# A one-core hybrid layer on Trainium2: buffers and priorities around the gates, the recurrence's decays and the first attention loads

## The chip, the cores and the metric

The kernel runs on one NeuronCore of one Trainium2 chip. The metric is the device time of one execution in microseconds (us). The engines that matter are the matrix engine TensorE (PE, with its weight loads shown apart as PEld), VectorE (DVE), ScalarE (ACT), GpSimd (POOL), and the queues that issue transfers: SyncE's (SP) and POOL's. Operands lie in the on-chip memory (SBUF), matmul results in PSUM, whose eight banks are shared out among pools of buffers.

## The reference

One layer of a streaming encoder over 512 tokens of width 1024, all in float32:

```python
h = rms_norm(x, norm_mix)
u_pool, u_lru, q, k, v, g_logits = split(h @ w_in)       # 1024 x 8192
gates = sigmoid(g_logits + b_gate)                        # three branches
y_pool = pool_mixer(u_pool)        # causal means over 2, 4, 8, 16 tokens, then a linear map
y_lru  = rglru_mixer(u_lru)        # width-4 conv, gates r and i, h = a*h + sqrt(1-a^2)*i*x
y_sb   = stick_breaking_attention(rms_norm(q), rms_norm(k), v)   # 8 heads of 128
merged = sum(gates[b] * (y_b @ w_branch[b]) for b in 3)
x = x + merged @ w_out
h2 = rms_norm(x, norm_ffn)
x = x + (silu(h2 @ w_ffn_gate) * (h2 @ w_ffn_up)) @ w_ffn_down   # width 2816
```

## The kernel before

Every float32 product is made of three matmuls in a rounded format: each operand is split into a high part (ACT copies it with rounding) and a low part (DVE subtracts the high part), and high*high, high*low and low*high are added up in PSUM. So each set of weights costs one transfer, one copy on ACT (`whi`, L141) and one subtraction on DVE (`wlo`, L142) before PE can use it; the weight pool `wp` has three buffers each for the raw weights, the high and the low parts. Some large products (q, k, v, the gates of branch 2, the projection of branch 2, most of the feed-forward) use a scheme of seven block products in place of eight, called "seven" in the code, with sums of blocks of weights and of inputs made on DVE or by adding transfers.

The program is written in order, stage by stage, and a scheduler puts it in order on each engine: it takes ready instructions by priority, which is the place in the program, and `tc.high_priority(n)` counts an instruction as n places earlier. A tile of a pool with a tag takes one of that tag's buffers, and its first writer waits until the buffer's last tile is done with. Small side tasks are put in two lists, `bg` and `abg`; `tick()`, called after every 12 or so matmuls of the main products, takes the next of each. The stages are:

1. Input scaling; gates of branch 0 (`gate_store`, L601); the scaled input `HH`, `HL`; block differences T1 to T4 (`prepare_t`, L568; `diff_h`, `split_t`).
2. The recurrent branch, four chunks of channels c: the projection (`lru_chunk`, L636), the convolution into `xc` (L642 to L651), its split (`xch`, `xcl`, L656, L657), the gate matmuls `lg` with tanh on ACT (L667 to L672), a tanh into `lt` (L679), the exponentials `lru_exp` (L697) and the root of the same tanh (L700, which needs another function table on ACT), the decay `lru_decay` (L705 and its complement, L707 on DVE for c < 2 and L709 on ACT for c of 2 and 3), the input (L713, L714), the scan (L720) and the store of its two halves (`lru_store`). Between the chunks the gates of branch 1 are made (`gate1`). The decay overwrites the tanh `t`, which the root has read before.
3. v, k and q as token-major products, in that order (`tok_product`, L827), with squares for the norms of k and q (`post`, L793); then the gates of branch 2 (`tx`, `ty`, L895).
4. The pool branch's projection in the group order 1, 0, 3, 2 (`pool_chunk`), whose results ACT copies out of PSUM (`evac_u`, L981) into slots, with the eight heads of attention as tasks in `abg` (`head_tasks`: the loads `at`, the transposes `pq`, the scores `z`, the transposes `pw`, the output `py`), followed by the projections of branches 1 and 0 (`branch`, L312 to L314 as `ps_br`), for which the recurrent branch's result is loaded into the space of HH and HL (L1196).
5. The projection of branch 2, the output projection, the feed-forward part.

In stages 1 to 3 the pool `ap0` holds tiles of 4 KB with the tags b (13 buffers), w (8) and t (8). The ring `m` of the pool `mp` has four such buffers and lives throughout; T1 to T4 use it first, later the merged branches. The space of `ap0` is taken by the slots and loads of stage 4 (`slot`, `slot_ld`) once the stages before are done.

High and low weights lie in buffers of 1152 elements, 128 more than they need; `OFF` and `STEPS` shift the start of the weights of certain products by 0, 4, 8, 12 and then 16 elements. An unused tile `pad` of 41 elements shifts all that lies behind it.

Of the kernel before, what the change touches and what calls it, by code (L numbers as in the profile page):

```python
# [16 lines left out]
P = 128  # L17
# [16 lines left out]
AHEAD = 200  # L34
PAD = 41


OFF = 16
STEPS = (0, 4, 8, 12)
NAW, NAT, NAB = 8, 8, 13  # L40
# [27 lines left out]
def layer_kernel(ctx: ExitStack, tc: tile.TileContext, x, xt, vecs, w_in, w_qkv7, w_gate7, w_pool, w_rg, w_ig,  # L68
# [6 lines left out]
    mp = ctx.enter_context(tc.tile_pool(name="mp", bufs=4))  # L75
    wp = ctx.enter_context(tc.tile_pool(name="wp", bufs=3))
    late = ctx.enter_context(ExitStack())
    hstack = ctx.enter_context(ExitStack())
# [50 lines left out]

    def weight_tiles(nh, nl, o=0):  # L130
        return [wp.tile([P, 1024 + 128], F32R, tag=tag, name=n)[:, o:o + 1024]
                for tag, n in (("whi", nh), ("wlo", nl))]

    def split_w(raw, shape, n, o=0):
        hi, lo = weight_tiles("whi" + n, "wlo" + n, o)
        if len(shape) == 3:
            hi, lo = (t.rearrange("p (a b) -> p a b", a=shape[1]) for t in (hi, lo))
        else:
            hi, lo = (t.rearrange("p (a b c) -> p a b c", a=shape[1], b=shape[2]) for t in (hi, lo))
        with tc.high_priority(60):  # L140
            act(hi, raw, AF.Copy)  # L141
            dve.tensor_tensor(lo, raw, hi.bitcast(F32), ALU.subtract)  # L142
        return hi, lo
# [58 lines left out]
    def add_seven(un, nm, i):  # L202
        u, pieces, shape = UNITS[un]
        last = i == pieces - 1

        def make(n):
            if nm == "S4":
                r = qraw[u, "12", i]
                dve.tensor_tensor(r, r, qraw[u, "S2", i], ALU.add)
            src = qraw[u, {"S1": "21", "S3": "11", "S4": "12"}.get(nm, nm), i]  # L210
            o = 0
            if u >= 3:
                o = goffs.pop(0) if goffs else OFF
            parts = split_w(src, [P] + list(shape), n, o)
# [12 lines left out]
            return parts  # L227
        specs.append((("seven", u, nm, i), make))

    goffs = list(STEPS)  # L230

# [28 lines left out]
    BNEXT = {"11": ("21", BY), "S1": ("11", BX), "S2": ("12", BX)}  # L260
    boffs = list(STEPS)

# [3 lines left out]
    def add_branch7(u, nm):  # L266
        def make(n):
# [3 lines left out]
            else:  # L271
                t = (BY if nm in ("11", "S3") else BX)[u]
            parts = split_w(t, [P, 2, 4, P], n, boffs.pop(0) if boffs else OFF)
            if nm in BNEXT:
# [19 lines left out]
    def emit_next():  # L294
        i = state["i"]
        if i >= len(specs):
            return
        state["i"] = i + 1
        key, make = specs[i]
        with tc.high_priority(AHEAD if i > 6 else 0):  # L300
            ready[key] = make(str(i))
# [30 lines left out]

    cst.tile([P, PAD], F32, tag="pad", name="pad")
    warm = cst.tile([P, S], BF16, tag="warm", name="warm")
    dve.memset(warm, 1.0)
# [108 lines left out]
    with ExitStack() as first:  # L444
# [12 lines left out]
        for i in range(WARM):  # L457
            nc.tensor.matmul(wps[:, 0, :], warm[:, 0:P], warm, start=True, stop=True)

# [141 lines left out]
        def gate_store(br, c, pss, scaled):  # L601
            gt = b4([2, S], f"gt{br}{c}")
            for j in range(2):
# [88 lines left out]
        def lru_exp(cs):  # L692
            for c in cs:
                for j in range(2):
                    r = lru[c]["r"][:, j, :]
                    ct = 2 * c + j
                    act(r, r, AF.Exp, scale=cneg[:, ct:ct + 1], bias=cneg[:, ct:ct + 1])  # L697
            for c in cs:
                lru[c]["s"] = b4([2, S], f"ls{c}")
                act(lru[c]["s"], lru[c]["t"], AF.Sqrt, scale=0.25)  # L700


        def lru_decay(c):
            e, t = lru[c]["r"], lru[c]["t"]
            dve.scalar_tensor_tensor(t, e, 1.0, t, ALU.add, ALU.mult)  # L705
            if c < 2:
                dve.tensor_scalar(t, t, -1.0, 1.0, ALU.mult, ALU.add)  # L707
            else:
                act(t, t, AF.Identity, scale=-1.0, bias=1.0)  # L709

# [5 lines left out]
        def lru_scan(c):  # L716
            t, s_ = lru[c]["t"], lru[c]["s"]
            h = lru[c]["i"]
# [34 lines left out]
        gate_store(0, 3, pss[3], False)  # L753
        tick(len(bg))

        def gate1(c):
# [22 lines left out]
        gate1(2)  # L779
        for f, c in ((lru_decay, 2), (lru_decay, 3), (lru_input, 2)):  # L780
            step(of(f, c))
        bg.extend(prepare_t())
        gate1(3)
# [9 lines left out]
        def post(t, i, j, r):  # L793
            if t < 2:
                sq = b4([2, 512], f"sq{t}{i}{j}")
                if t == 0:
# [97 lines left out]
        for cc in range(2):  # L894
            tx, ty = b4([2, S], f"gx{cc}"), b4([2, S], f"gy{cc}")  # L895
            if cc:
# [48 lines left out]
    with ExitStack() as mix:  # L945
# [34 lines left out]

        def evac_u(ps, name):  # L981
            u = slot(name)
            act(two(u), in_order(ps), AF.Copy)  # L983
            return u
# [35 lines left out]
        def pool_chunk(g):  # L1020
            pss = chan_chunk(("pool", g), hn, 1)
            us = [evac_u(pss[j], f"up{g}{j}") for j in range(2)]
            for j in range(2):
# [20 lines left out]
        def head_tasks(h):  # L1044
# [4 lines left out]
            def load():  # L1049
                for t in range(3):  # L1050
                    r = slot_ld(f"at{h}{t}", (NS, HD))
                    nc.sync.dma_start(r, qd[t, g][:, hd].rearrange("(b p) c -> p b c", p=P))
                    st["raw", t] = r
# [119 lines left out]
        def queue_attention():  # L1173
# [8 lines left out]
            for p in range(max(todo) + 1):  # L1182
                abg.append(lambda fs=todo.get(p, ()): [f() for f in fs])

        load_pool_weights(0)
        queue_attention()
        for g in POOL:
# [110 lines left out]
    with ExitStack() as ffn:  # L1298
# [114 lines left out]
        made = [0, NDIRECT]  # L1413
        offs = []

# [13 lines left out]
        def make_a(upto):  # L1429
            while made[0] < min(upto, len(steps)):  # L1430
                c, nm = steps[made[0]]
                made[0] += 1
                if (c, nm) == (NDIRECT, "11"):
                    offs.extend(STEPS)
                while made[1] < min(c + 2, DOWN):
# [5 lines left out]
        def split_a(src, n):  # L1441
            o = offs.pop(0) if offs else OFF
            h, l = (t.rearrange("p (w k c) -> p w k c", w=2, k=4)
                    for t in weight_tiles("wh" + n, "wl" + n, o))
            act(h, src, AF.Copy)  # L1445
# [133 lines left out]
        def make_d(upto):  # L1579
            while dmade[0] < min(upto, len(dsets)):  # L1580
                nm, n = dsets[dmade[0]]
                dmade[0] += 1
                if dmade[0] == 1:
                    offs.extend(STEPS)
                dfetch(dmade[0])
# [156 lines left out]
```

## Time and profile before

| | us |
|---|---|
| median of 3 runs | 871.64 |
| lowest, highest | 871.51, 872.29 |
| profiled execution, its time | 872.32 |
| profiled execution, its span in the trace | 870.5 |

The granted TensorE clock was full throughout. In the lines of the profile an engine's instruction is named by its line in the code (L142), its operation and its tiles, written as result<-operands; "[1.4 <-ACT up L983]" says that the engine had been idle for 1.4 us and what ended this. PEq, SPq and so on are the engines' queues. Times of PE's matmuls overlap, since they are pipelined: the distance from start to start is their pace.

### The profile page before, as it was taken

The numbers are of one execution on the slowest core, as the hardware profiler recorded it, in microseconds if no ns is written. First come the engines' busy times: TensorE is split into PE (matmuls) and PEld (weight loads), VectorE is DVE, ScalarE is ACT, GpSimd is POOL, SyncE is SP. The second block draws the span as 40 slices with busy tenths as digits, with TensorE's granted clock in tenths as the row PEclk, the third lists the DMA queues.
The fourth block names the chain that finished last, engine by engine and source line by source line (L and its number), as shares of the span: only waits on it lengthen the run. The fifth ranks groups of instructions, "written<-read, shape, count | busy, mean of one in ns | idle before, by whom it ended". The sixth has DMA issues, their size and how long they took to land.

```text
span 870.5 us, 14271 instructions
## 1 busy us (share of the span) xinstructions
PE 860.6 (99%) x5563; PEld 790.0 (91%) x5563; DVE 741.1 (85%) x961; ACT 523.1 (60%) x727; POOL 91.2 (10%) x130
## 2 busy tenths in 40 slices
PE   9999999999999999999999999999999999999998
PEld 7888878888899888889889998889999999999998
DVE  7899897998796599977988786699998888899974
ACT  7554989557966565565665545464555555755642
POOL 1110002232433101000001100000000000121200
PEclk9999999999999999999999999999999999999999
DMA  9586356798582886644636955345543433797913
GB/s 339 165 287 203 98 167 187 212 324 253 178 275 73 241 243 203 221 122 151 214 103 167 199 172 169 98 139 151 156 111 97 116 104 119 228 240 194 196 42 121
DMA packets 116643, 154.08 MB, mean 177 GB/s; under 512 B 8160, under 2 KB 90080, under 8 KB 116576
## 3 DMA queue, kind: packets, MB, share of 16 engines
q1 hardware_dynamic: 103904, 107.30, 38.4%
q0 software_dynamic: 12528, 45.62, 22.0%
q8 instruction: 43, 0.70, 0.3%
q10 hardware_dynamic: 144, 0.26, 0.1%
q14 instruction: 24, 0.20, 0.1%
HBM read 132.71 MB, written 18.87 MB: 174 GB/s over the span
## 4 chain that ended last, share of the span: by engine, by line
PE 84%; DVE 7%; ACT 5%; DMA 2%; issue 1%; SPq 0%; ACTq 0%; DVEq 0%
PE ps_y L321 11%; PE ps_x L321 8%; PE ps_q L837 7%; PE ps_dy L1661 6%; PE ps_dx L1661 5%; PE ps_br L312 3%; PE ps_br L313 3%; PE ps_br L314 3%; PE ps_bY L1280 2%; PE ps_gate L740 2%; PE ps_gy L321 2%; DVE wlo L142 2%; PE ps_bX L1280 2%; PE ps_gx L321 2%; PE ps_lru L312 1%; PE ps_out L312 1%
## 5 line engine op out<-in xcount | busy, mean ns | idle before, releaser
L141 ACT ACTIVATE whi<-raw 128x1024 fp32r<-128x1024 f32 x69 | 72.9, 1056 | 78.3 <-PE ps_out L313 16.1
L142 DVE TENSOR_TENSOR wlo<-raw,whi 128x1024 fp32r<-128x1024 f32 x69 | 84.3, 1221 | 24.8 <-ACT whi L141 24.3
L142 DVE TENSOR_TENSOR wlo<-qw,whi 128x1024 fp32r<-128x1024 f32 x48 | 58.4, 1220 | 16.5 <-ACT whi L141 16.3
L141 ACT ACTIVATE whi<-qw 128x1024 fp32r<-128x1024 f32 x48 | 50.6, 1054 | 28.8 <-PE ps_q L837 14.8
L1445 ACT ACTIVATE wh_S<-w_S 128x1024 fp32r<-128x1024 f32 x36 | 38.2, 1062 | 30.2 <-PE ps_y L321 18.3
L1565 POOL DMA_DIRECT2D dw<-in_w_down_dram x20 | 17.0, 864 | 306.1 <-DMA dw<-in_w_down_dram 263.8
L1446 DVE TENSOR_TENSOR wl_S<-w_S,wh_S 128x1024 fp32r<-128x1024 f32 x36 | 43.9, 1221 | 3.2 <-ACT wh_S L1445 3.2
L1445 ACT ACTIVATE wh<-w 128x1024 fp32r<-128x1024 f32 x27 | 28.6, 1060 | 29.3 <-PE ps_x L321 9.1
L1446 DVE TENSOR_TENSOR wl<-w,wh 128x1024 fp32r<-128x1024 f32 x27 | 33.0, 1221 | 8.2 <-ACT wh L1445 8.2
L1445 ACT ACTIVATE whdS<-dw 128x1024 fp32r<-128x1024 f32 x20 | 21.2, 1061 | 20.3 <-PE ps_dy L1661 11.2
L1096 DVE TENSOR_TENSOR_SCAN E<-K,ahead 128x512 f32<-128x512 f32 (+3 forms) x32 | 25.4, 814 | 3.9 <-ACT K L1092 3.9
L1446 DVE TENSOR_TENSOR wldS<-dw,whdS 128x1024 fp32r<-128x1024 f32 x20 | 24.2, 1222 | 4.9 <-ACT whdS L1445 4.9
L312 PE MATMUL ps_br<-yHH,whi 128*128 128x512 f32 x64 | 24.6, 385 | 1.4 <-ACT up L983 1.4
L312 PE MATMUL ps_lru<-HH,whi 128*128 128x512 f32 x64 | 24.6, 384 | 0.0
L312 PE MATMUL ps_br<-yph,whi 128*128 128x512 f32 x64 | 24.5, 383 | 0.0
L312 PE MATMUL ps_pool<-HH,whi 128*128 128x512 f32 x64 | 24.5, 383 | 0.0
L312 PE MATMUL ps_gate<-HH,whi 128*128 128x512 f32 x64 | 24.4, 381 | 0.0
L313 PE MATMUL ps_lru<-HL,whi 128*128 128x512 f32 x64 | 24.3, 379 | 0.0
L314 PE MATMUL ps_lru<-HH,wlo 128*128 128x512 f32 x64 | 24.3, 379 | 0.0
L313 PE MATMUL ps_gate<-HL,whi 128*128 128x512 f32 x64 | 24.3, 379 | 0.0
L314 PE MATMUL ps_gate<-HH,wlo 128*128 128x512 f32 x64 | 24.3, 379 | 0.0
L313 PE MATMUL ps_pool<-HL,whi 128*128 128x512 f32 x64 | 24.3, 379 | 0.0
(740 smaller groups left out, 3444.5 us busy)
## 6 DMA issues: line engine op xcount, KB each, us to landing
raw<-in_w_in_dram SPq DMA_DIRECT2D x31, 512.0 KB, 5.3
qw<-in_w_qkv_dram SPq DMA_DIRECT2D x24, 512.0 KB, 6.8
dw<-in_w_down_dram POOLq DMA_DIRECT2D x20, 512.0 KB, 9.2
w<-in_w_ffn_gate_dram SPq DMA_DIRECT2D x36, 256.0 KB, 3.7
w<-in_w_ffn_up_dram SPq DMA_DIRECT2D x36, 256.0 KB, 4.2
raw<-in_w_branch_dram SPq DMA_DIRECT2D x16, 512.0 KB, 3.9
qw<-in_w_qkv_dram POOLq DMA_DIRECT2D x12, 512.0 KB, 8.1
qd<-r POOLq DMA_DIRECT2D x12, 512.0 KB, 6.7
```

The lines of the kernel that those rows point to most:

```text
L141: act(hi, raw, AF.Copy)
L142: dve.tensor_tensor(lo, raw, hi.bitcast(F32), ALU.subtract)
L312: nc.tensor.matmul(ps, lh, rh, start=start, stop=False, skip_group_check=skip)
L313: nc.tensor.matmul(ps, lh, rl, start=False, stop=False, skip_group_check=skip)
L314: nc.tensor.matmul(ps, ll, rh, start=False, stop=stop, skip_group_check=skip)
L321: nc.tensor.matmul(o, a_[a][:, w, k, :], il2(b_[b][:, k, :]), start=first and n == k == 0, stop=last and n == 2 and k == 3, skip_group_che ...
L837: nc.tensor.matmul(ps[:, a, :], b_[:, k, ts_], il(a_[:, kk, :]), start=first and n == k == 0, stop=n == 2 and k == 3, skip_group_check=True)
L1096: dve.tensor_tensor_scan(E[:, c0:c0 + n][:, ::-1], K[:, c0 + 1:c0 + n + 1][:, ::-1], ahead[:, S - n:][:, ::-1], 0.0, ALU.mult, ALU.add)
L1280: nc.tensor.matmul(o, ah[x_][:, w, k, :], il2(b[k][y_]), start=first_ and n == k == 0, stop=n == 2 and k == 3, skip_group_check=True)
L1445: act(h, src, AF.Copy)
L1446: dve.tensor_tensor(l, src, h.bitcast(F32), ALU.subtract)
L1661: nc.tensor.matmul(o, a_[a][:, w, k0 + k, :], il2(b_[b][:, k, :]), start=first and i == k == 0, stop=last and i == 2 and k == nk - 1, skip ...
```

## The change

- The tiles of branch 1's gates (`gt`) and the squares (`sq`) come from the ring `m` in place of tag b. T1 to T4 and their splits are made right after the gates of branch 0 in the program, ahead of the recurrent branch; they stood behind its third gate chunk.
- For chunks 2 and 3 the first step of the decay is made between the exponentials and the roots, into a buffer of its own (`la`); the root then overwrites the tanh, where it had a buffer `ls`. The complement on ACT becomes a step of its own, where the whole decay was.
- Weights of v get an advance of 320 places in place of 200.
- A new outer pool `ex` with two buffers of 2 KB holds the first two loads of attention (q and k of head 0, with an advance of 400) and later the copies of the last pool chunk (with an advance of 300). The attention tasks are queued before the first pool weights are loaded, and the first of them, head 0's loads, is taken at once, so each following task comes one tick sooner.
- The second pair of `gx`, `gy` comes from tag w.
- For space, the shifts of the weights, their 128 spare elements and `pad` go, and the warm-up matmuls read a tile of 128 columns four times over in place of one of 512.

```diff
-PAD = 41
-OFF = 16
-STEPS = (0, 4, 8, 12)
...
+    ex = ctx.enter_context(tc.tile_pool(name="ex", bufs=2))
...
-    def weight_tiles(nh, nl, o=0):
-        return [wp.tile([P, 1024 + 128], F32R, tag=tag, name=n)[:, o:o + 1024]
+    def weight_tiles(nh, nl):
+        return [wp.tile([P, 1024], F32R, tag=tag, name=n)
...
-        with tc.high_priority(AHEAD if i > 6 else 0):
+        with tc.high_priority((320 if key[:2] == ("seven", 2) else AHEAD) if i > 6 else 0):
...
-    cst.tile([P, PAD], F32, tag="pad", name="pad")
-    warm = cst.tile([P, S], BF16, tag="warm", name="warm")
+    warm = cst.tile([P, P], BF16, tag="warm", name="warm")
...
-            nc.tensor.matmul(wps[:, 0, :], warm[:, 0:P], warm, start=True, stop=True)
+            nc.tensor.matmul(wps[:, 0, :], warm, warm.unsqueeze(1).to_broadcast([P, 4, P]), start=True, stop=True)
...
-            gt = b4([2, S], f"gt{br}{c}")
+            gt = mp.tile([P, 2, S], F32, tag="m", name=f"gt{br}{c}") if br else b4([2, S], f"gt{br}{c}")
...
+            if len(cs) > 1:
+                for c in cs:
+                    lru_decay(c)
             for c in cs:
-                lru[c]["s"] = b4([2, S], f"ls{c}")
-                act(lru[c]["s"], lru[c]["t"], AF.Sqrt, scale=0.25)
+                st = lru[c]
+                st["s"] = st["t"] if "a" in st else b4([2, S], f"ls{c}")
+                act(st["s"], st["t"], AF.Sqrt, scale=0.25)
...
         def lru_decay(c):
             e, t = lru[c]["r"], lru[c]["t"]
-            dve.scalar_tensor_tensor(t, e, 1.0, t, ALU.add, ALU.mult)
+            a = lru[c]["a"] = t if c < 2 else b4([2, S], f"la{c}")
+            dve.scalar_tensor_tensor(a, e, 1.0, t, ALU.add, ALU.mult)
             if c < 2:
-                dve.tensor_scalar(t, t, -1.0, 1.0, ALU.mult, ALU.add)
-            else:
-                act(t, t, AF.Identity, scale=-1.0, bias=1.0)
+                dve.tensor_scalar(a, a, -1.0, 1.0, ALU.mult, ALU.add)
+
+        def lru_complement(c):
+            a = lru[c]["a"]
+            act(a, a, AF.Identity, scale=-1.0, bias=1.0)
...
         tick(len(bg))
+        for f in prepare_t():
+            f()
...
-        for f, c in ((lru_decay, 2), (lru_decay, 3), (lru_input, 2)):
+        for f, c in ((lru_complement, 2), (lru_complement, 3), (lru_input, 2)):
             step(of(f, c))
-        bg.extend(prepare_t())
...
-                sq = b4([2, 512], f"sq{t}{i}{j}")
+                sq = mp.tile([P, 2, 512], F32, tag="m", name=f"sq{t}{i}{j}")
...
-            tx, ty = b4([2, S], f"gx{cc}"), b4([2, S], f"gy{cc}")
+            tx, ty = (b4([2, S], f"g{n}{cc}", "bw"[cc]) for n in "xy")
...
-        def evac_u(ps, name):
-            u = slot(name)
-            act(two(u), in_order(ps), AF.Copy)
+        def evac_u(ps, name, last):
+            u = ex.tile([P, S], F32, tag="u", name=name) if last else slot(name)
+            with tc.high_priority(EARLY if last else 0):
+                act(two(u), in_order(ps), AF.Copy)
...
-                    r = slot_ld(f"at{h}{t}", (NS, HD))
-                    nc.sync.dma_start(r, qd[t, g][:, hd].rearrange("(b p) c -> p b c", p=P))
+                    with tc.high_priority(400 if h == 0 and t < 2 else 0):
+                        r = (ex.tile([P, NS, HD], F32, tag="u", name=f"at{h}{t}") if h == 0 and t < 2
+                             else slot_ld(f"at{h}{t}", (NS, HD)))
+                        nc.sync.dma_start(r, qd[t, g][:, hd].rearrange("(b p) c -> p b c", p=P))
...
-        load_pool_weights(0)
         queue_attention()
+        abg.pop(0)()
+        load_pool_weights(0)
```

More of the change, by code (lines that the diff above doesn't have):

```diff
@@ L127, in halves, with split_w @@
         return [t[:, 0:2, :], t[:, 2:4, :]]
-    def weight_tiles(nh, nl, o=0):
-        return [wp.tile([P, 1024 + 128], F32R, tag=tag, name=n)[:, o:o + 1024]
+    def weight_tiles(nh, nl):
+        return [wp.tile([P, 1024], F32R, tag=tag, name=n)
                 for tag, n in (("whi", nh), ("wlo", nl))]
-    def split_w(raw, shape, n, o=0):
-        hi, lo = weight_tiles("whi" + n, "wlo" + n, o)
+    def split_w(raw, shape, n):
+        hi, lo = weight_tiles("whi" + n, "wlo" + n)
         if len(shape) == 3:
@@ L210, in make @@
             src = qraw[u, {"S1": "21", "S3": "11", "S4": "12"}.get(nm, nm), i]
[L211 to L214, printed above, removed]
+            parts = split_w(src, [P] + list(shape), n)
             if nm == "11":
@@ L228, in add_seven @@
         specs.append((("seven", u, nm, i), make))
-    goffs = list(STEPS)
     def add_then(f):
@@ L260, in layer_kernel @@
     BNEXT = {"11": ("21", BY), "S1": ("11", BX), "S2": ("12", BX)}
-    boffs = list(STEPS)
     def bsrc(u, nm):
@@ L272, in make @@
                 t = (BY if nm in ("11", "S3") else BX)[u]
-            parts = split_w(t, [P, 2, 4, P], n, boffs.pop(0) if boffs else OFF)
+            parts = split_w(t, [P, 2, 4, P], n)
             if nm in BNEXT:
@@ L716, in lru_scan @@
         def lru_scan(c):
-            t, s_ = lru[c]["t"], lru[c]["s"]
+            t, s_ = lru[c]["a"], lru[c]["s"]
             h = lru[c]["i"]
@@ L1021, in pool_chunk @@
             pss = chan_chunk(("pool", g), hn, 1)
-            us = [evac_u(pss[j], f"up{g}{j}") for j in range(2)]
+            us = [evac_u(pss[j], f"up{g}{j}", g == POOL[3]) for j in range(2)]
             for j in range(2):
@@ L1183, in queue_attention @@
                 abg.append(lambda fs=todo.get(p, ()): [f() for f in fs])
+        queue_attention()
+        abg.pop(0)()
         load_pool_weights(0)
-        queue_attention()
         for g in POOL:
@@ L1413, in layer_kernel @@
         made = [0, NDIRECT]
-        offs = []
         def load_a(c):
@@ L1432, in make_a @@
                 made[0] += 1
-                if (c, nm) == (NDIRECT, "11"):
-                    offs.extend(STEPS)
                 while made[1] < min(c + 2, DOWN):
@@ L1441, in split_a @@
         def split_a(src, n):
-            o = offs.pop(0) if offs else OFF
             h, l = (t.rearrange("p (w k c) -> p w k c", w=2, k=4)
-                    for t in weight_tiles("wh" + n, "wl" + n, o))
+                    for t in weight_tiles("wh" + n, "wl" + n))
             act(h, src, AF.Copy)
@@ L1582, in make_d @@
                 dmade[0] += 1
-                if dmade[0] == 1:
-                    offs.extend(STEPS)
                 dfetch(dmade[0])
```

## The prediction, made before the changed kernel ran

> **What bounds the kernel now.** I read the page's head first, then the waits of TensorE, then the order of time on ACT, DVE, PE and the queues around each wait.
>
> ```profile
> span 870.5 us, 14271 instructions
> PE 860.6 (99%) x5563; PEld 790.0 (91%) x5563; DVE 741.1 (85%) x961; ACT 523.1 (60%) x727; POOL 91.2 (10%) x130
> ```
>
> ```profile
> PE warm_ps L458 <- DVE warm L335: 1.5, 1, 1.5
> PE ps_br L312 <- ACT up L983: 1.4, 1, 1.4
> PE lg L667 <- DVE xcl L657: 1.4, 1, 1.4
> PE ps_q L837 <- DVE wlo L142: 1.2, 3, 0.7
> PE ps_q L837 <- ACT r L850: 0.5, 1, 0.5
> ```
>
> The matmuls fill the span. No part of the change adds or removes a matmul (nine warm-up matmuls keep their count and width), so it can gain only what PE loses in waits. The waits column is: who waited for whom, us in all, times, longest. The first is the warm-up; the other four make 4.5 us, 0.5% of the span. That is the prize; what can be lost is open. I price each wait.
>
> **The change part by part: the last pool chunk's copies (1.4 us).**
>
> ```profile
> 345.46 0.56 POOL L1196 DMA_DIRECT2D yHL<-ydl  x1
> DMA to landing us min/median/max: 8.5/8.5/8.5
> 344.36 0.63 ACT L941 ACTIVATE p31h<-up 128x512 fp32r<-128x512 f32 x1 [3.55 <-DVE up L997]
> 349.12 1.10 ACT L983 ACTIVATE up<-ps_pool 128x512 f32<-128x512 f32 x2
> 349.79 0.48 PE L312 MATMUL ps_br<-yHH,whi 128*128 128x512 f32 x1 [1.44 <-ACT up L983]
> 352.48 0.71 PE L1109 MATMUL pw<-idn,A 128*128 128x128 f32 x5
> ```
>
> Three PSUM buffers hold the pool and branch chunks, two to a chunk, so the second half of the first branch chunk waits until ACT has copied the pool chunk out. ACT made both copies at 349.12 although it stood idle for 3.55 us before 344.36. With two buffers of their own and a priority of 300 the copies need no free slot and can fill that idle time: minus 1.4. What is late next is the last load of yHL: issued at 345.46, landed 8.5 later at 354.0. It reads into the space of HL, so it cannot start before the last pool matmul, and it doesn't move. Without the wait PE would come to the next half chunk at about 351.0, but the attention queue now runs one tick ahead (first task popped at once), which puts the ten transposes at 352.48, six score matmuls and the next head's eight transposes in front of it: about 2.8 us at the rates below, so 353 to 354. Bounds: minus 1.4 to nothing. I take minus 1.4, as the inserted work covers the landing; if it falls behind instead, up to 1.4 comes back.
>
> **The attention loads (0.4 us).**
>
> ```profile
> 229.59 17.40 SPq L198 DMA_DIRECT2D qw<-in_w_gate_dram  x8
> 285.63 6.35 SPq L148 DMA_DIRECT2D raw<-in_w_in_dram  x3
> 292.14 3.55 SPq L1052 DMA_DIRECT2D at<-qd  x4
> 253.93 0.75 POOL L790 DMA_DIRECT2D qd<-r  x1 [2.90 <-DVE r L854]
> 299.12 0.63 PE L1059 MATMUL pq<-idn,at 128*128 128x128 f32 x4
> 299.93 0.66 PE L1059 MATMUL pq<-idn,at 128*128 128x128 f32 x4 [0.18 <-DMA at<-qd]
> 458.40 1.09 PE pw L1109 x10
> ```
>
> Ten transposes take 1.09 us, so four take 0.44; here 0.81 passes before the second four: 0.4 lost to the loads issued at 292.14. In outer buffers with priority 400 the q and k loads of head 0 no longer need the space of the first stage. Their source is stored by 253.93, and SP issues nothing between about 247 and 285.63, so if they wait at SP's head for that store, nothing that PE needs soon is behind them; the raw loads of L148 come later. Minus 0.4. The other bound: the transposes now come one tick (12 matmuls, 2.6 us) sooner; were the loads not sooner, the wait would be 3.0, so plus 2.6. The idle SP speaks for minus 0.4.
>
> **Decays ahead of the roots, v's weights (1.2 us).**
>
> ```profile
> 133.28 2.92 ACT L697 ACTIVATE lr<-lr,cneg 128x512 f32<-128x512 f32 x4
> 137.17 1.28 ACT L700 ACT_TABLE_LOAD   x1
> 138.47 2.00 ACT L700 ACTIVATE ls<-lt 128x1024 f32<-128x1024 f32 x2
> 140.49 1.28 ACT L609 ACT_TABLE_LOAD   x1
> 137.19 1.23 DVE L142 TENSOR_TENSOR wlo<-qw,whi 128x1024 fp32r<-128x1024 f32 x1 [2.55 <-ACT whi L141]
> 139.56 1.23 DVE L705 SCALAR_TENSOR_TENSOR lt<-lr,lt 128x1024 f32<-128x1024 f32 x1 [1.14 <-ACT ls L700]
> 142.97 1.22 DVE L705 SCALAR_TENSOR_TENSOR lt<-lr,lt 128x1024 f32<-128x1024 f32 x1
> 158.87 2.33 DVE L720 TENSOR_TENSOR_SCAN li<-lt,ls 128x512 f32<-128x512 f32 x2
> 161.12 1.20 DVE L142 TENSOR_TENSOR wlo<-qw,whi 128x1024 fp32r<-128x1024 f32 x1
> 140.00:150.00 10.00, 9.76 (x45) 8.23 (x44) 10.00 (x10) 9.97 (x13) 2.50 (x3) 1.00 0.65 129
> 150.00:160.00 10.00, 9.77 (x45) 8.23 (x44) 10.00 (x9) 5.83 (x6) 1.48 (x2) 1.00 0.61 213
> ```
>
> The last two rows are windows: length, then busy PE, PEld, DVE, ACT, POOL, clock, DMA. From 140 to 160 DVE is full and the three waits for v's split weights fall there and just after. Today the decays of chunks 2 and 3 overwrite the tanh that the roots read, so they follow the roots, at 139.56 and 142.97, into the full stretch. In their own buffers they need only the exponentials, done by 136.2, and fit into DVE's idle 2.55 before 137.19: 2 x 1.2 = 2.4 us of DVE leave the full stretch. The longest lateness is a split behind two scans at 158.87; with 2.4 less ahead it clears. The advance of 320 instead of 200 adds little: a split can't start before PE frees one of three buffers, it only chooses among ready work. Minus 1.0 of the 1.2. The change adds a wait: the roots overwrite the tanh in place, so ACT stands at the root until the decay is done, and behind it stand the table load, the gate's copies and v's splits. The decays should end by about 137.6 and the first root stands at 138.47. The other bound: the second decay is late and the two roots are parted by a tanh, two more table loads, 2 x 1.28 = plus 2.6.
>
> [...]
>
> **Buffers for branch 1's gates (1.4 us), the differences, squares, gx and gy.**
>
> ```profile
> 107.99 1.22 DVE L705 SCALAR_TENSOR_TENSOR lt<-lr,lt 128x1024 f32<-128x1024 f32 x1 [2.36 <-ACT ls L700]
> 110.87 1.52 DVE L642 TENSOR_SCALAR xc<-ps_lru,vt 128x512 f32<-128x512 f32 x2
> 121.38 1.22 DVE L657 TENSOR_TENSOR xcl<-xc,xch 128x1024 fp32r<-128x1024 f32 x1
> L560 DVE SCALAR_TENSOR_TENSOR hT<-hT,xt x4: 682/682/684, 52.6 to 55.7; 128x512 f32<-128x512 f32 x4
> ```
>
> Chunk 3's convolution starts at 110.87, after 2.36 idle and other work, and its split ends late for the gates' matmuls. Gates in the merge ring give back one to two of 13 buffers here. That may let the chain into the idle time (minus 1.4) or change nothing, as the order on DVE was settled by the scheduler; one operation more ahead would be plus 1.2. I take the middle of gain and nothing: minus 0.7. The differences T1 to T4 are moved far forward in the program, yet the trace has them at 52 to 56 already, as fillers: nothing. They empty the merge ring long before branch 1's first gate needs it. Squares and gx, gy: nothing. The shorter warm tile starts the warm-up a little sooner, and the first real matmul waits for its data: nothing.
>
> **The weights' start offsets go.**
>
> ```profile
> 251.20 2.68 PE ps_gy L321 x24
> 264.60 2.68 PE ps_gx L321 x24
> 362.26 0.28 PE L312 MATMUL z<-qkh,qkh 128*128 128x256 f32 x1
> 362.48 0.28 PE L314 MATMUL z<-qkh,qkl 128*128 128x256 f32 x1
> ```
>
> The first product has weights at offset 0, that at 264.60 at 64 bytes; both take 2.68 for 24, 111.7 ns each. In z both operands come from slots of equal size, so they lie alike, as weights and factors will: two in 0.22, the same. Nothing. The other bound: 111.7 stands 2.4 ns above the 109 of a transpose; were that step paid again on the 3,024 such products (1,512 in the feed-forward, 336 gate, 336 branch, 840 down, counted from the loops), plus 7.3.
>
> **The sum.** Minus 1.4, 0.4, 1.0 and 0.7, plus 0.5 (my estimate, one wait of the size of that for r) for a wait that a new order makes: minus 3.0. The profiled execution took 872.32 (span 870.5), so 869.3; it lies 0.68 above the median of the runs, 871.64, so I predict 868.6. All four waits gone and the loads' 0.4 is minus 4.9: 866.7.
>
> **The rivals.** *Only the outer buffers work*: the DVE order stays, minus 1.8, 869.8. For it: the scheduler placed DVE's work by priorities, not by this trace. Against it: decays freed of the roots must move. *Roots parted on ACT*: plus 2.6 in place of minus 1.0, no gain at the convolution; minus 1.4 and 0.4 stay, so plus 0.8: 872.4. For it: ACT is 9.97 of 10 busy from 140; against: the decays' idle time is there. *Loads no earlier*: plus 2.6 for minus 0.4, 871.6; against it speaks the idle SP. *Slower, by addresses*: all split weights and their factors lie alike modulo their size, the 256-column products pay 2.4 ns more, minus 3.0 plus 7.3: 875.9. It decides from 1.0 ns a product (3.0 / 3,024). Against it stand z and the equal rates at offsets 0 and 64 bytes; for it, that PEld is 91% busy, with no room. *A worse order*: the same lists are sorted anew, and one split queued behind two more scans (2.33) at each of the three places where wlo is late today is plus 7.0 less 3.0: 875.6, at two of them 873.3.
>
> **How the numbers follow.** Forecast 0.58 (own range 867 to 870), only outer buffers 0.10, roots parted 0.07, loads late 0.03, addresses 0.10, worse order 0.12. A difference under 0.2%, 1.7 us, can't be told from none. Faster: 0.58 and half of the 0.10, 0.63; same: the other half, 0.07 and 0.03, 0.15; slower 0.22. Low end 866.4, just under all waits gone; high end 874.6, past the worse order at two places, which leaves the rest of that case and the addresses' full price out.
>
> **What would show it.** Right: copies `up` before 346 and no wait of ps_br; head 0's q and k loads before 285; both L705 of the last chunks before the roots and no wait for wlo from 140 to 165; 2.68 for 24 products everywhere. Wrong: table loads between the two roots, a wait of ps_br for yHL at 352 to 354, a pq wait of 2 us or more, or a product at other than 111.7 ns.

## The result and the profile after

The changed kernel takes 879.66 us (median of 6 runs, 878.3 to 881.8) where the kernel before takes 871.58 in the same comparison: ratio 1.0096, interval 1.0081 to 1.0112, so 8.1 us slower. Its profiled execution took 881.58 (span 879.8), 1.9 above that median.

Where the time is lost can be read from the first matmul of each stage (us from the start of the span, profiled executions):

| first matmul of | before | after | lost by then |
|---|---|---|---|
| recurrent branch, `ps_lru` | 48.3 | 48.6 | 0.3 |
| v, k, q, `ps_q` | 139.6 | 141.2 | 1.6 |
| gates of branch 2, `ps_gy` | 251.0 | 254.3 | 3.3 |
| pool, attention, branches, `ps_pool` | 288.6 | 293.3 | 4.7 |
| projection of branch 2, `ps_bY` | 471.5 | 481.4 | 9.9 |
| down projection, `ps_dy` | 772.8 | 782.7 | 9.9 |

About half goes in stages 1 to 3, half in stage 4, nothing behind it. Of the 9.3 us between the two spans, 7.0 are waits: all that PE's list has sums to 13.9 after and 6.9 before. Another 1.7 went to a slower clock (last section). PE's waits of the changed kernel (what waits, for what; us in total, times, longest):

```profile
PE pw L1111 <- DVE ypl L1011: 4.2, 3, 2.0
PE ps_q L836 <- DVE wlo L140: 2.3, 4, 1.0
PE lg L658 <- DVE xcl L648: 1.7, 1, 1.7
PE ps_gy L313 <- ACT gx L912: 1.3, 1, 1.3
...
PE lg L658 <- DVE xch L647: 1.0, 1, 1.0
```

The wait of `ps_br` for the copies `up` is gone, as forecast, and so is that of `pq` for the loads. But `pw` for `ypl`, the largest, is new, as are those for `xch` and `gx`, and `pq` waits 1.1 for `wtl` where it waited 0.2. Most of the steps that the prediction wanted to see did happen; the waits for `wlo` between 140 and 165 did not go (1.2 us, three times). The timeline after (start, duration, engine and line, operation; in brackets the idle time before it):

```profile
132.95 1.22 DVE L701 SCALAR_TENSOR_TENSOR la<-lr,lt 128x1024 f32<-128x1024 f32 x1
...
136.48 1.23 DVE L701 SCALAR_TENSOR_TENSOR la<-lr,lt 128x1024 f32<-128x1024 f32 x1
...
137.76 1.06 ACT L695 ACTIVATE lt<-lt 128x1024 f32<-128x1024 f32 x1
138.72 1.04 ACT L139 ACTIVATE whi<-qw 128x1024 fp32r<-128x1024 f32 x1
139.67 1.04 ACT L695 ACTIVATE lt<-lt 128x1024 f32<-128x1024 f32 x1
...
257.89 1.84 SPq L1054 DMA_DIRECT2D at<-qd  x2
...
301.09 1.04 PE L1061 MATMUL pq<-idn,at 128*128 128x128 f32 x8
...
345.87 0.59 ACT L983 ACTIVATE up<-ps_pool 128x512 f32<-128x512 f32 x1
...
349.89 0.58 ACT L983 ACTIVATE up<-ps_pool 128x512 f32<-128x512 f32 x1
```

Both decays (`la`) start ahead of the roots, between which there is a copy but no table load. The first loads are issued at 257.89, where they stood at 292.14, and the eight transposes `pq` run in one piece. The copies `up` come at 345.87 and 349.89, ahead of the branch's first product at 350.2. So four steps went as planned, and the time was lost beside them. How, in stage 4, the timeline of the changed kernel shows around the first new wait:

```profile
350.02 0.38 PE L306 MATMUL pps<-p01h,wpl 128*128 128x512 f32 x1
...
353.53 0.69 DVE L997 SCALAR_TENSOR_TENSOR up<-pw,up 128x512 f32<-128x512 f32 x1
354.26 0.63 ACT L940 ACTIVATE p31h<-up 128x512 fp32r<-128x512 f32 x1 [3.79 <-DVE up L997]
354.80 0.67 ACT L1010 ACTIVATE yph<-pps,vt 128x512 fp32r<-128x512 f32 x1
355.53 0.74 DVE L1011 SCALAR_TENSOR_TENSOR ypl<-pps,vt,yph 128x512 fp32r<-128x512 f32 x1
...
356.42 0.52 PE L1111 MATMUL pw<-idn,A 128*128 128x128 f32 x3 [1.96 <-DVE ypl L1011]
...
378.82 0.64 PE L1111 MATMUL pw<-idn,A 128*128 128x128 f32 x3 [2.01 <-DVE ypl L1011]
```

Read it from below. `pw`, the transposes of the attention factors, wait for one of the three small PSUM buffers that they share with the pool products `pps`, `pq` and `py`. It comes free when ACT (`yph`) and DVE (`ypl`) have read `pps`. ACT could have done so long before: the last product `pps` starts at 350.02 and takes 0.38, but from then on ACT stands for 3.79 us at `p31h`, the split of another pool group's mean, which DVE ends only at 354.2, and `yph` lies behind it in ACT's queue. With the tick kept (e2 and e4 below) no wait of `pw` for `ypl` is listed.

ACT took nothing past the head of its queue here: it was idle for 3.79 us at `p31h`, with `yph` behind it, whose product `pps` was done at about 350.4 (350.02 and 0.38); `yph` ran at 354.80.

### The profile page after: what moved, and what is told of

It reads as the page before. It is cut to its first block, busy times and chain, and to the rows that moved or that the text cites. A ratio compares the mean times of both kernels' runs of the same rounds, so it can differ in the third digit from the quotient of the medians.

```text
span 879.8 us, 14273 instructions
## 1 busy us (share of the span) xinstructions
PE 862.7 (98%) x5563; PEld 791.2 (90%) x5563; DVE 741.9 (84%) x961; ACT 521.5 (59%) x727; POOL 91.1 (10%) x130
## 4 chain that ended last, share of the span: by engine, by line
PE 71%; DVE 12%; ACT 7%; DMA 5%; issue 4%; POOL 1%; DVEq 0%; POOLq 0%; ACTq 0%
PE ps_y L313 11%; PE ps_x L313 8%; PE ps_dy L1658 6%; PE ps_dx L1658 5%; DVE wlo L140 4%; DMA qw<-in_w_qkv_dram 3%; PE ps_br L305 3%; PE ps_br L306 3%; PE ps_br L304 3%; PE ps_gate L738 2%; PE ps_bY L1283 2%; PE ps_gy L313 2%; PE ps_bX L1283 2%; PE ps_gx L313 2%; DMA qw<-in_w_gate_dram 1%
## 5 line engine op out<-in xcount | busy, mean ns | idle before, releaser
L305 PE MATMUL ps_br<-yHL,whi 128*128 128x512 f32 x64 | 24.6, 384 | 0.0
L1094 ACT ACTIVATE K<-z,qrs 128x512 f32<-128x512 f32 (+3 forms) x32 | 16.9, 529 | 12.9 <-PE z L306 10.7
L306 PE MATMUL ps_br<-yHH,wlo 128*128 128x512 f32 x64 | 24.6, 384 | 0.0
L305 PE MATMUL ps_br<-ypl,whi 128*128 128x512 f32 x64 | 24.3, 380 | 0.0
```

The source lines that it names most:

```text
L305: nc.tensor.matmul(ps, lh, rl, start=False, stop=False, skip_group_check=skip)
L306: nc.tensor.matmul(ps, ll, rh, start=False, stop=stop, skip_group_check=skip)
```

## The experiments

All were timed in three rounds (five for the last three), each against the kernel before on the same chip; before had medians of 871.58 to 871.94. The chips differ between e1 to e8, e9 to e12 and e13 to e15. Each is told as a difference to the changed kernel or to another run.

| run | median, us | ratio to before, interval |
|---|---|---|
| e1_offsets_only | 871.74 | 0.9996, 0.9987 to 1.0005 |
| e2_outer_only | 871.58 | 0.9995, 0.9986 to 1.0005 |
| e3_tick_early | 876.35 | 1.0049, 1.0034 to 1.0064 |
| e4_tick_kept | 875.61 | 1.0035, 1.0026 to 1.0045 |
| e5_decays_only | 871.38 | 0.9998, 0.9989 to 1.0007 |
| e6_gates_only | 873.83 | 1.0027, 1.0015 to 1.0040 |
| e7_four_small_buffers | 877.19 | 1.0062, 1.0047 to 1.0077 |
| e8_mean_one_tick_later | 873.21 | 1.0012, 1.0003 to 1.0021 |
| e9_splits_behind | 874.19 | 1.0030, 1.0017 to 1.0042 |
| e10_squares_back | 873.51 | 1.0022, 1.0013 to 1.0031 |
| e11_means_together | 873.50 | 1.0020, 1.0008 to 1.0033 |
| e12_three_decays | 873.11 | 1.0010, 1.0001 to 1.0019 |
| e13_means_and_splits | 871.28 | 0.9996, 0.9987 to 1.0005 |
| e14_with_three_decays | 870.96 | 0.9993, 0.9984 to 1.0002 |
| e15_splits_between | 870.37 | 0.9982, 0.9973 to 0.9991 |

**Which half costs what: e1 to e4.** e1 is the kernel before without the shifts, spare elements and `pad`, and with the short warm-up tile. e2 adds the outer buffers, with an empty task in place of the tick that the change takes ahead. e3 is e2 without this empty task. e4 is the whole change with it:

```diff
         queue_attention()
         abg.pop(0)()
+        abg.insert(0, nothing)
         load_pool_weights(0)
```

> The kernel before with the weights' shifts, their spare elements and the pad gone and the short warm-up tile, nothing else. Every engine keeps its order. Theory (addresses cost nothing, the loss is in the order of work): 871.6, within 0.7, and 2.68 us for 24 of the 256-column products. Rival (addresses cost): 875 or more, with a pace over 112 ns.

> e1 plus the two outer buffers, the early q and k loads of head 0 and the early copies of the last pool chunk; every later attention task keeps its tick. Theory: the wait of ps_br for up and the wait of pq go, minus 1.8, so 869.8. Rival (these copies or loads disturb something): 871.6 or more.

> e2 with the first attention task taken at once, so that every task comes one tick sooner, as in the changed kernel. Theory (the transposes of the attention weights then meet the pool branch's results in the three small PSUM buffers): 5 to 7 us over e2, 875 to 877, with waits of pw for ypl between 350 and 380. Rival (the changes of the stages before cause the loss): within 1 us of e2.

> The changed kernel with one empty task in the attention queue, so that every task comes at its old tick; the loads stay early. Theory (about half of the loss is the tick, half stands in the stages before the pool chunks, which begin 4.8 us later in the changed kernel's trace): 873 to 875, no wait of pw for ypl. Rival (all of the loss is the tick): 870. Rival (none of it): 879.

e1 came out at 871.74: the start addresses cost nothing, and that rival falls. e3 against e2 is 4.8 us: the one earlier tick alone. e4 against e2 is 4.0: the rest of the change. e2 plus both would be 880.4, and the changed kernel has 879.7, so they add up. (e4's 875.61 lies above its expected 873 to 875; its ten runs spread from 873.9 to 877.2.) e2 itself gained nothing (871.58), although its list has no wait for `up`. Its own new wait in PE's list:

```profile
PE pq L1053 <- DVE wtl L1106: 1.7, 2, 1.5
```

And in the timeline of e2 what DVE does ahead of it:

```profile
351.77 0.15 DVE L983 COPY pw<-up 128x1 f32<-128x1 f32 x1
...
353.42 0.68 DVE L984 TENSOR_TENSOR pw<-pw 128x508 f32<-128x508 f32 x1
...
355.16 1.61 DVE L1106 TENSOR_TENSOR wtl<-pw,wth 128x512 fp32r<-128x512 f32 x3
```

Because `up` comes early, DVE can start the means (L983, L984: 351.77 to 354.02) and does so ahead of `wtl`, on which a small buffer hangs. The 1.4 us are saved at one place and 1.5 are paid 6 us later.

**Which edit costs the 4.0 of stages 1 to 3: e5, e6, e10.** e5 is e2 with the decays and the advance of 320, e6 is e2 with the gates in the ring `m` and the differences queued at once, e10 is e4 with the squares back in tag b:

```diff
-                sq = mp.tile([P, 2, 512], F32, tag="m", name=f"sq{t}{i}{j}")
+                sq = b4([2, 512], f"sq{t}{i}{j}")
```

> The kernel of e2_outer_only (871.6) with the two last decays in buffers of their own ahead of the roots, and with the longer advance for v's weights; gates, squares, gx and gy stay in their old buffers. What stands open after e4_tick_kept (875.6) is which edit of the first three stages costs its 4.0 us. Theory G: it is branch 1's gates in the merge ring, by the new order of ACT and DVE around chunk 3. Then this run shows 870.4 to 871.6: the split weights from 140 to 165 are no longer late (up to 1.2 less) and lg waits 1.3 for xcl as before. Theory D: the decays ahead of the roots cost it, as 2.4 us of DVE ahead of the split of chunk 3; then 875, with lg waiting 2.7 in all.

> The kernel of e2_outer_only (871.6) with branch 1's gates in the merge ring and the differences queued at once; decays, advance and squares as before. Theory G: 875, with lg waiting for xch and xcl 2.7 us in all and some of the k stage's waits. Theory D: 871.6 with lg waiting 1.3. If both this and e5 lie near 873.5 the cost is shared; if both lie near 871.6 the two cost only together, or the squares cost it.

> The kernel of e4_tick_kept (875.6) with the squares back in their old buffers. e6_gates_only took 2.3 us more than e2, so 1.7 of the 4.0 of the first three stages are not the gates'. Theory S: it is the squares, which share the four merge buffers with the gates and shift ACT and DVE in the k stage (waits for wlo at 222 and 229 us, 2.0 us, in e4, none in e6). Then 873.8, and these two waits are gone. Rival: it is the decays and the gates together; then 875.6 with both waits.

e5 shows no loss and no gain; the split weights that it should have made punctual are as late as before (`ps_q` for `wlo`: 1.4 us in its list, 1.2 in e2's). e6 costs 2.3 us against e2, less than the whole that theory G gave it, and e10 shows 2.1 for the squares against e4. The two sum to 4.4, of 4.0: theory G holds for about half, theory S for the other half, theory D falls. The squares' share is the less certain: e4 and e10 ran on two chips, and by their ratios it is 1.1. The traces speak for 2.4: from the first `ps_lru` to the first `ps_pool` e4 takes 244.1 us, e10 241.7, e2 240.2. e6 has two edits in one, but the differences stay where they were (`hT` from 51.5 us in e6, 51.0 in e2, and the whole run is 0.4 later), so the cost is most likely the gates'. (The run e10 also had no wait for `wlo` at 222 and 229 us, as expected; e4 had two.)

How gates in other buffers delay a convolution: the timeline of e2 around chunk 3.

```profile
112.61 1.06 ACT L139 ACTIVATE whi<-raw 128x1024 fp32r<-128x1024 f32 x1
113.70 1.23 DVE L140 TENSOR_TENSOR wlo<-raw,whi 128x1024 fp32r<-128x1024 f32 x1 [0.30 <-ACT whi L139]
...
120.97 1.22 DVE L648 TENSOR_TENSOR xcl<-xc,xch 128x1024 fp32r<-128x1024 f32 x1
121.26 1.25 ACT L600 ACTIVATE gt<-ps_gate,bhalf 128x512 f32<-128x512 f32 x2
```

The same stretch in the timeline of e6:

```profile
115.22 2.00 ACT L139 ACTIVATE whi<-raw 128x1024 fp32r<-128x1024 f32 x2
116.31 1.23 DVE L140 TENSOR_TENSOR wlo<-raw,whi 128x1024 fp32r<-128x1024 f32 x1 [1.19 <-ACT whi L139]
117.13 1.25 ACT L600 ACTIVATE gt<-ps_gate,bhalf 128x512 f32<-128x512 f32 x2
117.45 2.56 DVE L642 SCALAR_TENSOR_TENSOR xc<-ps_lru,vt,xc 128x2 f32<-128x2 f32 x7
...
122.79 1.22 DVE L648 TENSOR_TENSOR xcl<-xc,xch 128x1024 fp32r<-128x1024 f32 x1
```

With a free buffer the gates `gt` are made 4.1 us sooner (117.13 for 121.26), though only their store waits for them. ACT's whole order shifts, the copy `whi` comes at 115.22 for 112.61, and DVE stands 1.19 us at `wlo`, with the rest of chunk 3's convolution behind it. `xcl` starts 1.8 later, and `lg` waits 2.7 in all where it waited 1.3. The squares do the same to ACT in the k stage (timeline of e4):

```profile
222.82 1.06 ACT L802 ACTIVATE sq<-r 128x1024 f32<-128x1024 f32 x1 [3.17 <-DVE r L853]
223.79 1.04 ACT L139 ACTIVATE whi<-qw 128x1024 fp32r<-128x1024 f32 x1
```

The same square and the same copy in the timeline of e10:

```profile
217.65 1.06 ACT L802 ACTIVATE sq<-r 128x1024 f32<-128x1024 f32 x1 [1.34 <-DVE r L853]
218.61 1.04 ACT L139 ACTIVATE whi<-qw 128x1024 fp32r<-128x1024 f32 x1
```

In e4 the square stands at the head for 3.17 us, until DVE has made its `r`, and the copies of the next weights stand behind it; in e10 it stands for 1.34. Of the 5.2 us between the two copies, 2.3 are a later start (e4's profiled execution has its first `ps_q` at 144.4, e10's at 142.1) and 0.5 an earlier wait of e4 for `wlo`; the rest arises here. The wait of `ps_gy` for `gx` in the changed kernel has the same form, a square with `gx` behind it on ACT:

```profile
258.51 1.06 ACT L796 ACTIVATE sq<-r 128x1024 f32<-128x1024 f32 x1 [2.92 <-DVE r L853]
...
260.43 0.58 ACT L912 ACTIVATE gx<-ps_gy 128x512 f32<-128x512 f32 x1
```

e9 has this wait too; e4, e7 and e10, with `gx` in the same buffers, have not.

And why the decays gave nothing: the timeline of e2 where v's third late split stands.

```profile
158.43 2.34 DVE L711 TENSOR_TENSOR_SCAN li<-lt,ls 128x512 f32<-128x512 f32 x2
160.68 1.21 DVE L140 TENSOR_TENSOR wlo<-qw,whi 128x1024 fp32r<-128x1024 f32 x1
```

The same place in the timeline of e5:

```profile
155.43 1.22 DVE L718 TENSOR_TENSOR_SCAN li<-la,lt 128x512 f32<-128x512 f32 x1
...
157.68 3.45 DVE L718 TENSOR_TENSOR_SCAN li<-la,lt 128x512 f32<-128x512 f32 x3
161.04 3.47 DVE L140 TENSOR_TENSOR wlo<-qw,whi 128x1024 fp32r<-128x1024 f32 x3
```

DVE had the 2.4 us back, and its order filled them with two more scans ahead of the same split (one at 155.43, and three for two behind it). The split starts at 161.04 for 160.68, which is the 0.4 by which all of this run is later.

**What the early tick hangs on: e7 and e9.** e7 gives the small PSUM ring a fourth buffer (taken from the scores), e9 leaves the buffers and moves the splits of the means behind the pool products of the chunk before:

```diff
-            pool_p.setdefault(g, []).append(split_hl(u, f"p{g}{j}"))
...
             if g != POOL[0]:
                 queue_pool_back(POOL[POOL.index(g) - 1])
+            last = bg.pop()
+            bg.append(lambda: (last(), pool_p.__setitem__(
+                g, [split_hl(us[j], f"p{g}{j}") for j in range(2)])))
```

> The changed kernel (879.7) with four small PSUM buffers in place of three, and one for the scores in place of two. Theory R (the transposes pw, one tick early, wait for a buffer that the pool products still hold): two of the three pw find a buffer at once, the third waits for the first ypl only, so the waits of pw for ypl fall from 4.2 to under 1.5 and the time to about 876. Rival (ACT standing at p31h is the cost, whatever the buffers): the pw waits end but the wait moves to the next reader (pq or py), and the time stays at 879 to 880. A price of its own would be a wait of z for its single buffer, some 0.5 us for each of 24 scores at most; then above 880.

> The changed kernel (879.7), with the splits of a pool chunk's means taken out of the task of the mean and put behind the pool products of the chunk before, so that ACT has the copies yph ahead of p30h and p31h. After e7, where a fourth buffer left 3.5 of the 4.2 us, theory A: the buffer is late because ACT stands at p31h, at the head of its queue, until DVE has finished the mean, and yph lies behind it. Then the waits of pw for ypl fall to under 1 us in all, and the time by that and the lost clock, to 874.9 to 876. Rival B: one tick is too short for the copies whatever stands ahead of them; the waits stay at 3 us or more and the time at 878 to 880.

In e7 the wait of `pw` for `ypl` stayed at 3.5 of 4.2: theory R falls (the rival's shift of the wait to `pq` or `py` didn't come either; it stayed where it was). The time is 2.5 lower all the same; 1.3 of it is the wait of `ps_gy` for `gx`, which its list lacks, and another 1.3 the waits of `ps_q` for `wlo` (1.0 for 2.3), as the order moved there too. In e9 the waits of `pw` for `ypl` are gone and the time is 874.19, 5.5 below the changed kernel and a little below the expected 874.9 to 876. From the first `ps_pool` to the first `ps_bY` e9 takes 182.5 us where the changed kernel takes 188.1 and e2 182.9, so this edit gives back the whole cost of the tick. ACT's timeline there, for comparison with that at 354:

```profile
348.97 0.69 ACT L1009 ACTIVATE yph<-pps,vt 128x512 fp32r<-128x512 f32 x1
...
350.60 0.61 ACT L940 ACTIVATE p30h<-up 128x512 fp32r<-128x512 f32 x1
351.12 0.62 ACT L940 ACTIVATE p31h<-up 128x512 fp32r<-128x512 f32 x1
```

The copy `yph` goes ahead of the splits and nothing stands. So theory A holds: the tick cost what it did because of what stood ahead of `yph` on ACT, not because of the number of buffers.

**Can the 1.4 us at `ps_br` be kept: e8, e11, e13, e15.** Four orders of the last pool chunk's means, splits and products, all with the tick kept; e12 is e11 with e5's decays and also chunk 1's decay ahead of its root, and e14 and e15 build on e12's stages 1 to 3. The edits of the last chunk, one after the other:

```diff
 e8   the means one task later, and the products with them
+            if g == POOL[3]:
+                bg.extend([nothing] * 1)
 e11  both means in the second of their two tasks
+                means = [nothing, lambda ms=means: [m() for m in ms]]
 e15  e13's splits, for the last chunk, in the task before (index -2 for -1)
+            at = -1 if g != POOL[3] else -2
```

e13 is e11's means with e9's splits (for all chunks). The edit for chunk 1's decay, in e12, e14 and e15:

```diff
-            if len(cs) > 1:
+            if 0 not in cs:
...
-            a = lru[c]["a"] = t if c < 2 else b4([2, S], f"la{c}")
+            a = lru[c]["a"] = t if c < 1 else b4([2, S], f"la{c}")
```

> The kernel of e2_outer_only (871.6), with the last pool's means queued one tick later, so that DVE takes wlo and the three wtl ahead of them. Theory: in e2 the early copies let DVE do 2.3 us of pool means ahead of wtl, and pq waited 1.5 (1.9 between starts) for the buffer that wtl still read; with wtl first the 1.4 saved at ps_br stays saved: 869.9. Rival: the means and the pool products behind them come a tick later and another wait takes the place: 871.6, or 873 if the branch 0 products wait for the pool's outputs.

> The kernel of e2_outer_only (871.6), with both means of the last pool chunk in the second of their two ticks, so that wlo and the three wtl stand ahead of them on DVE; the pool products keep their ticks, which e8 had moved by one, with a wait of 2.5 us of pw for ypl. Theory: the wait of pq for wtl (1.5, 1.9 between starts) goes and none takes its place: 869.9. Rival: the means, 2.3 to 4.6 us later, make the last pool products or their copies late: 871 to 873.

> The kernel of e5_decays_only (871.4) with the means of e11, and with the decay of chunk 1 too in a buffer of its own ahead of its root, so that DVE need not wait 2.4 us for that root ahead of chunk 3's convolution. If both work: 869.9 less up to 1.3 at lg, 868.6. If the order of ACT that this makes (the root of chunk 1 and its two table loads move behind chunk 2's gates) costs as much as the merge ring's did: 872 or more, with lg waiting over 2 us.

> The kernel of e11_means_together (873.5), with the splits of the means behind the pool products of the chunk before, as in e9_splits_behind. Theory A: each wait of this stage comes from an engine that stands at the head of its queue for a mean (in e11 ACT at p20h, with the copy ysb behind it, 3.0 us of pps); with means behind wtl and splits behind yph and ysb the 1.4 us of ps_br stay saved: 869.9 to 870.3. Rival B: the three small PSUM buffers give the time back whatever the order: 871.5 to 873.5, with a wait of 1 us or more at pq, pw or pps between 345 and 380.

> The kernel of e13_means_and_splits with the three decays ahead of their roots and the advance of e12_three_decays. In e12 the wait of lg was gone (1.3) and waits for wlo after 142 us gave back 0.8, so 0.5 below e13: 869.4 if theory A holds there, 871 to 873 if rival B does. The same as e13 or more would say that the decays' gain doesn't reach the end.

> The kernel of e14_with_three_decays (871.0), with the splits of the last pool chunk one task sooner, between the two pool products of the chunk before. Theory A: the wait of pps for p20l (1.3, 1.6 between starts) is an order on DVE; the splits end 1.3 us sooner, the wait goes, and the time is 869.5. Rival: the second ypl is now late for pw, or the chain from the copies is as long as its cover, and 870.7 to 872 comes out, with a wait of another name between 365 and 385.

e8 and e11 failed, as their rivals said: the wait of `pq` went, and `pw` waited 2.5 for `ypl` in e8, `pps` 3.0 for `ysb` in e11. The timeline of e11 shows the pattern of 354 again:

```profile
370.63 0.63 ACT L932 ACTIVATE p21h<-up 128x512 fp32r<-128x512 f32 x1 [4.75 <-DVE up L989]
371.17 0.58 ACT L1120 ACTIVATE ysb<-py 128x512 f32<-128x512 f32 x1
```

With the splits moved behind (e13), only `pps` for `p20l` was left of it, 1.3; e13 stayed at 871.28, so neither of its theories has it whole: the wait of the ring went, and the splits themselves were late. One task sooner for the last chunk's (e15), and the wait of 1.3 falls to two short ones in PE's list:

```profile
PE pps L305 <- DVE p20l L943: 0.4, 1, 0.4
...
PE pps L305 <- DVE p21l L943: 0.3, 1, 0.3
```

In e12 `lg` no longer waits (1.3 before), and 0.7 of it comes back at `wlo`; the 2.6 of `pps` for `ysb`, e11's wait, keeps its time high (873.11 for an expected 868.6): its first product of stage 3 starts at 137.6 for e11's 139.2, its `ps_gy` at 250.1 for 250.6. Neither e12 against e11 nor e14 against e13 (870.96, 871.28) resolves it in the times. e14's 870.96 missed its expected 869.4. e15, with all of it, takes 870.37, between its theory (869.5) and its rival (870.7 to 872); its ratio to before is 0.9982 with an interval that leaves out 1, 1.2 us by the medians. It is the one version here that is faster than the kernel before beyond the noise; against e14 alone the 0.6 isn't. What it keeps of the change are the outer buffers, the decays, v's advance and the dropped shifts; gates, differences, squares, `gx`, `gy` and the tick are undone.

## Why the prediction was wrong

It forecast 868.6, with a range from 866.4 to 874.6, and the kernel takes 879.7. Step by step:

- *Copies of the last pool chunk, minus 1.4.* The mechanism was right (they come at 345.87, no wait for `up`), the sum wrong: DVE used the early data to put the means ahead of `wtl`. The step asked what the copy frees, not what the free engine starts next. e15 is faster by 1.2 with an order to fit, so a gain was there; how much of it comes from the copies isn't shown alone.
- *Loads of head 0, minus 0.4, other bound plus 2.6 if the loads were late.* Loads and `pq` went as forecast. The earlier tick is the step that failed most: the prediction followed it to the loads and, as welcome cover, to PE's order before the last load of yHL, and put no price on the three small PSUM buffers. Moving `abg` by one tick against `bg` brought `pw` up to `pps` in the ring that they share. Measured, plus 4.8 (e3 against e2).
- *Decays and v's weights, minus 1.0.* They moved as forecast, without table loads between the roots (137.76 and 139.67; the loads, 1.28 us each, stand at 136.46 and 140.72); the gain was zero (e5), since two scans took the place. The sentence "with 2.4 less ahead it clears" held everything else on DVE fixed.
- *Gates in the merge ring, minus 0.7.* The bounds were minus 1.4 and plus 1.2; plus 2.3 was measured (e6). The bound allowed for one DVE operation more, not for ACT's order and a DVE that stands behind it.
- *"Squares and gx, gy: nothing."* Plus 2.1 for the squares (e10 against e4). Here no price was set where one was needed; for `gx`, `gy` no run stands alone, but e10, which has them, takes 873.51 and e6, which has not, 873.83.
- *Start addresses, nothing.* Right (e1); the 256-column products of the changed kernel keep 2.68 us for 24 (from 261.27).
- *New order, plus 0.5.* Mis-sized by the most: the waits that new orders made, with the clock lost behind one of them, are nearly all of the 8 us. The rival "a worse order" had the kind of cause, but put it at v's weights with 7.0; the places were chunk 3's convolution, the k stage and the small PSUM ring.

## What to carry to other kernels

When a change frees a buffer or makes data early, ask what each engine will start with it, and what then stands behind the head of its queue: three edits here that only gave buffers or moved a task made ACT or DVE stand 1.2 to 3.8 us at an operand that was not ready. Two lists of tasks that share a ring of buffers keep their distance for a reason; moving one against the other by a single task needs the ring's readers written out. And a saved wait counts only once the next wait on the same engine has been looked for, a few microseconds further on.

## What was not expected of the hardware

Some waits of PE cost more than their length: behind them the granted clock fell, for 1.7 us each time. The changed kernel's windows right behind the second wait of `pw` (length, busy PE, PEld, DVE, ACT, POOL with counts, then the clock, DMA share, GB/s):

```profile
378.00:382.00 4.00, 3.18 (x13) 3.02 (x14) 3.91 (x7) 3.31 (x7) 0.00 (x0) 0.64 0.05 7
382.00:386.00 4.00, 4.00 (x19) 3.37 (x19) 2.81 (x5) 1.79 (x4) 0.00 (x0) 0.93 0.36 124
```

Matmuls at the end of that stretch, in PE's timeline:

```profile
381.29 0.63 PE L304 MATMUL ps_br<-yHH,whi 128*128 128x512 f32 x1
381.71 0.63 PE L305 MATMUL ps_br<-yHL,whi 128*128 128x512 f32 x1
...
382.56 0.38 PE L304 MATMUL ps_br<-yHH,whi 128*128 128x512 f32 x1
382.78 0.38 PE L305 MATMUL ps_br<-yHL,whi 128*128 128x512 f32 x1
```

After 2.0 us of idle PE the starts are 0.42 apart until 382.56, then 0.22: half the pace for some 3.4 us (in finer windows the clock is 0.64 from 379.0 to 379.5, 0.50 from 379.5 to 382.5, 0.94 from 382.5 to 383.0 and 1.00 behind that). The same stands behind the first wait of `pw` in e3 (1.96 us, until 351.0): from 352 to 356 its clock is 0.58, and 0.998 over the whole execution.

Over a whole profiled execution the mean clock is 0.998 in the changed kernel, e3, e4, e8, e9, e10 and e12, 0.996 in e7, and 1.000 in the others. By windows of 4 us these are nine places, two of them in e7. Each stands right behind waits of PE that sum to 2.0 to 2.7 us within 5 us, for `pw`, `pps` or `lg`, and each costs 1.7 us (the window's length times the share of the clock that is missing). It isn't certain: the first such wait of the changed kernel, at 356.42, had matmuls 0.22 apart right behind it (clock 1.00 from 356 to 360), its 2.7 us at `lg` and those of e6 left the clock at 1.00, and so did e11's 3.0 us. Between runs of one kernel the same is seen: of e11's ten runs the five with a mean clock of 1.000 took 872.0 to 873.2, the five with 0.996 to 0.998 took 873.8 to 876.4. The changed kernel's six runs all lie at 0.996 to 0.998; my estimate from this is that 1.8 to 3.5 us of its time (0.2% to 0.4% of 880) are lost clock, where the kernel before was profiled at 1.000.

So 2.0 us of idling at one place were followed by half the pace (0.42 from start to start), and 3.0 us at another were not; what decides between the two no run here shows.
